# Tiles of 512 bytes and more on 128-byte borders of their SBUF partition

## Chip, cores and metric

The kernel runs on one core of a Trainium2 chip. The metric is the device time of one execution in microseconds (us), as the median of several runs. SBUF has 128 partitions. A tile `[P, n]` of float32 takes 4n bytes at the same place of each partition, and "start" means in all that follows the first byte of such a place modulo 128.

## What is computed

The reference runs x, a 256 x 1024 float32 array, through four blocks: twice the first kind, a final norm, twice the second kind. Cut to what matters:

```python
for l in range(2):                                    # first kind
    x = x + 0.5 * swiglu(rms_norm(x), w_gu, w_down)   # 1024 -> 2 x 2816 -> 1024
    x = x + hybrid_mixer(rms_norm(x))   # gated spatial unit + top-k attention, gated, @ w_out
    x = x + 0.5 * swiglu(rms_norm(x), w_gu, w_down)
x = rms_norm(x)
for l in range(2):                                    # second kind
    h = hybrid_mixer_2(rms_norm(x))     # gated delta rule + dilated attention, @ w_out
    x = x + rms_norm(h)
    h = conv_glu(rms_norm(x))           # up, convolution over 3 tokens, gelu gate, down
    x = x + rms_norm(h)
```

All products are wanted to float32 accuracy.

## The kernel before

Activations lie with features on the partitions and the 256 tokens along the partition, in chunks of 128 features. Weights come from DRAM in slabs of 128 x 1024 (4 KB of each partition) by DMAs that the SP queue issues (`raw`, L179), into four buffers `wraw`.

Each slab is split into two float32r parts: ScalarE writes the rounded part `whi` (`act`, L144), and VectorE and GpSimd write the rest `wlo`, 640 and 384 columns of it (`tt`, L161). Activations are split in the same way into `[P, 2, 256]` tiles: `h` out of the norms, `hid` for the hidden chunks of the feed-forward blocks, `ya`, `yb` and `zh` in the first mixer, `oa` and `ob` in the second.

`mm3_steps` (its product is at L222) makes one 128 x 256 output from 8 such chunks with three products a chunk: `whi` by the first part and `wlo` by the first part in turns, then `whi` by the second part. In each, the 128 x 128 block of the weight slab is loaded into the array as the stationary operand (512 bytes of a partition), and the activation part streams past it as the moving operand (1024 bytes). The trace shows the load as PEld and the product as PE. The load of the next product runs while the present one streams. `token_steps` (L542 to L544) has the roles the other way: 512 columns of the weights move past a block of `h`. Products of plain float32 (transposes, attention scores, the delta rule) have two records of PE each.

A feed-forward stage is an up part (44 slabs of 24 products with `h` as the moving operand) and a down part (8 outputs from 22 chunks, 8 x 66 = 528 products with `hid` moving). There are four SwiGLU stages (`swiglu`) and two with a convolution (`conv_glu`).

**Where tiles start.** A pool (`tc.tile_pool`) hands out places one behind the other, in the order in which names are first asked for. Each place is rounded up to 32 bytes and there are as many places as the name has buffers. Pools open at the same time lie one behind the other. The first pool begins at a multiple of 128. So the starts follow from the code:

- `const`: 352 + 512 + 32 + 64 + 2080 + 32 + 32 + 1024 = 4128 bytes, so that the next pool begins at 32.
- `weights` (4096 x 4 x 3 bytes) and `state`: `wraw`, `whi`, `wlo`, `x`, `sq`, `h`, `ssum`, `rb` start at 32. `state` ends with small tiles of 192 bytes in all, and what follows begins at 96.
- `const1`, `const2` (tables), and the pools `ffn` and `glu`: all start at 96, `t`, `s`, `p`, `y` and `hid` among them.
- `mix1`: `lng`, `ws`, `cosr`, `rm2s`, `k`, `q`, `qi`, `ya` at 96; `rl` and `score` at 32; `yb` and `zh` at 64.
- `mix2`: the 2 KB tiles of the delta rule (`big`, which later hold `obh` and `obl`), `pm2s`, `qT`, `vT`, `sz` at 96; `ct`, `Tf`, `XTf` (later `oa`), `rope` at 64; `kT` and `qg` at 0; `ob` at 32.

A block of a weight slab starts 512 bytes behind the block before it, and the second part of an activation 1024 bytes behind the first, so all blocks and parts of a tile have the tile's start. Of the products of L222, stationary and moving operand therefore start at: `h` 32 and 32; `hid` and `ya` 32 and 96; `yb`, `zh` and `oa` 32 and 64; `ob` 96 and 32.

What sets the order of the work is written in the kernel (`manual_schedule` around the mixers' products) or left to the scheduler of the tile framework. Neither is touched.

Of the kernel before, what the change touches and what calls it, by code (L numbers as in the profile page):

```python
# [7 lines left out]
F32 = mybir.dt.float32  # L8
# [3 lines left out]
PSUM = bass.MemoryType.PSUM  # L12
# [5 lines left out]
P = 128  # L18
T = 256
# [18 lines left out]
# how much other work the tensor engine gets in each wait of the second mixer  # L38
# [4 lines left out]
# columns of the per-partition vectors  # L43
# [5 lines left out]

class Kernel:  # L50
    def __init__(self, tc, ctx, I, out):
        self.tc, self.nc, self.I, self.out = tc, tc.nc, I, out
        pool = lambda **k: ctx.enter_context(tc.tile_pool(**k))
        self.cp = pool(name="const", bufs=1)
        self.wp = pool(name="weights", bufs=4)
        self.sp = pool(name="state", bufs=2)
        self.pp = pool(name="acc", bufs=4, space=PSUM)

    # ---------------------------------------------------------------- the whole
    def run(self, stages=None):  # L60
# [25 lines left out]
        with self.tc.tile_pool(name="const1", bufs=1) as cp:  # L86
            con = self.vec2 = None
            for n, (kind, l) in enumerate(first):
                if n == 1:
                    self.second_constants()  # L90
                v = vec1[:, 8 + V1 * l:8 + V1 * (l + 1)]
                if kind == "mixer1":
                    if con is None:
                        con = {n: self.load(cp, list(I[n].shape), I[n], n)
                               for n in ("cos1", "sin1", "causal0", "causal1")}
                        self.cos1, self.sin1 = con["cos1"], con["sin1"]
                        self.causal = [con["causal0"], con["causal1"]]
                    self.mixer1(l, v)
                else:
                    g = V_FFN1 if kind == "ffn1" else V_FFN2  # L100
                    self.swiglu(v[:, g:g + 8], I[kind + "_gu"][l], I[kind + "_down"][l])
# [3 lines left out]
        with self.tc.tile_pool(name="const2", bufs=1) as cp:  # L105
# [33 lines left out]
    # ---------------------------------------------------------------- small helpers  # L139
# [6 lines left out]
    def turn(self):  # L146
        """Functions of one table come in turns on the scalar engine: what act_next issues from
        here on stays behind what it issued before."""
        self.before, self.latest = self.latest, None
# [32 lines left out]
    def piece(self, src, n, pool_cols=None):  # L182
        """A slab of weights in its two exact float32r parts."""
        if self.plan or self.made:
            while self.plan and len(self.made) < 3:
                self.made.append(self.parts(*self.plan.pop(0)))
            for p in self.plan[len(self.ahead):self.far]:
                self.ahead.append(self.raw(p[0], p[1]))
            return self.made.pop(0)
        return self.parts(src, n, pool_cols)  # L190
# [21 lines left out]
    def mm3(self, ps, w, hs, start=True, stop=True, M=P):  # L212
        """ps[m, t] += W^T h for a slab of len(hs) blocks of M columns."""
# [3 lines left out]
    def mm3_steps(self, ps, w, hs, start=True, stop=True, M=P, shared=False):  # L217
        """The same a product at a time. In a bank shared by two open sums the one that begins first
        has start; that marks the whole bank as unwritten."""
# [14 lines left out]
    def pump(self, us):  # L234
        """Issue that much of the products that wait in the queue."""
# [6 lines left out]
    def split(self, pool, src, name, bufs, lo_eng=None, tag=None):  # L242
        """src (SBUF, float32) in its two float32r parts."""
# [5 lines left out]
    # ---------------------------------------------------------------- normalisation  # L249
# [5 lines left out]
    def square_sum(self, acc, src, **k):  # L255
        """Sum of squares over chunks: a pair of addends, of which the second is the latest."""
# [9 lines left out]
    def rms(self, acc, n):  # L266
        """1/sqrt(mean + eps) by token: on the partitions [128, 2], and along the free axis in PSUM."""
# [3 lines left out]
    def warm(self, n, of=None):  # L271
        """Products for nothing: the tensor engine's clock would halve in a long wait."""
# [16 lines left out]
    def column_sums(self, ps, acc, first, warm=0):  # L289
        """ps[t, b] = sum over the partitions, for the tokens of each block; first: opens the bank."""  # L290
# [14 lines left out]
    def norm(self, g):  # L305
        """x * g in two parts by chunk of features, and 1/rms by token (applied after the product)."""
# [34 lines left out]
    def between(self, gf, g):  # L341
        """x = rmsnorm(x) * gf, then what scaled(g) gives for it; the first norm's scale by token joins
        the second's, so that the products need not wait for either."""
# [27 lines left out]
        def column():  # L371
# [7 lines left out]
            # the mean square of the normed x  # L379
# [15 lines left out]
    def add_normed(self, ys, acc, g=None):  # L395
        """x += rmsnorm(y) * g', for ys = y * g'; then what scaled(g) gives for the new x."""
# [40 lines left out]
    # ---------------------------------------------------------------- gated feed-forward  # L437
    def swiglu(self, g, wgu, wd):
# [3 lines left out]
        with self.tc.tile_pool(name="ffn", bufs=2) as fp:  # L442
# [20 lines left out]
    def open_pairs(self, w, hs, column):  # L463
        """The first two pairs of products, feature chunk by feature chunk as they come from the norm."""
# [19 lines left out]
    def conv_glu(self, vec, wup, wdown, following):  # L484
# [4 lines left out]
        with self.tc.tile_pool(name="glu", bufs=2) as fp:  # L489
# [34 lines left out]
    # ---------------------------------------------------------------- projections  # L524
    def token_layout(self, src, hs, parts=4):
        """The 512 columns of a projection with tokens on the partitions: two banks."""
# [27 lines left out]
    def rotated(self, pool, ps, cs, tag, swaps, m2s):  # L554
        """ps * cos + partner(ps) * sin; the partner rows come by DMA."""
# [11 lines left out]
    # ---------------------------------------------------------------- softmax attention  # L567
    def attention(self, pool, q, k, v, bias, tag, fill=0.0, outs=None, midway=None):
        """8 heads of 64; bias by block of queries: [128, keys]. Out: 4 chunks [c, t] in two parts."""
# [5 lines left out]
        def scores(u):  # L575
            pp, qb, e = u
            nk = P * (qb + 1)
            # two heads on the same rows of the array
# [61 lines left out]
    # ---------------------------------------------------------------- the first block's mixer  # L640
    def selection(self, pool, qi, ki, wt):
        """The bias that keeps, for each query, the top 64 keys by the indexer's score, causally."""
# [32 lines left out]
    def mixer1(self, l, vec):  # L675
# [16 lines left out]
        mp = self.tc.tile_pool(name="mix1", bufs=1)  # L692
        swaps = [(64 * a + 32 * b, 64 * a + 32 * (1 - b), 32) for a in range(2) for b in range(2)]
        with mp as mp:
# [20 lines left out]
            # the indexer: queries, one key, head weights  # L715
# [22 lines left out]
            # the gated spatial unit  # L738
# [36 lines left out]
            # attention over the selected keys  # L775
# [7 lines left out]
            # the gates' products fill the waits  # L783
# [36 lines left out]
    def rows(self, ap, n):  # L820
        """A vector of DRAM on every partition."""
        return bass.AP(tensor=ap.tensor, offset=ap.offset, ap=[[0, P], [1, n]])

    # ---------------------------------------------------------------- the second block's mixer
    def mixer2(self, l, vec, following):
# [15 lines left out]
        with self.tc.tile_pool(name="mix2", bufs=1) as mp, self.tc.manual_schedule(engines={PE}):  # L841
            # keys, beta and decay: feature chunk by feature chunk, as they come from the norm
# [5 lines left out]
            for d in range(KD):  # L848
                for g in sums:
                    next(g), next(g)  # L850
                # the two parts of the weights side by side
# [21 lines left out]
            def silu(y):  # L873
                # the exponentials come before all of these
# [5 lines left out]
            def conv_steps(ps, c0, out, name):  # L880
                """A causal convolution over four tokens, then silu, for two chunks."""
# [61 lines left out]
            # what fills the tensor engine in the waits of the delta rule  # L943
# [45 lines left out]
            def delta_part():  # L989
                for m in range(KD):  # L990
                    w = self.piece(None, 0)
                    # the other half of the weights waits in tiles that the delta rule has left
# [45 lines left out]
class Delta:  # L1038
    """The gated delta rule over chunks of 64 tokens, two chunks to a block of 128."""
# [21 lines left out]
    def inverse_norms(self, x, name):  # L1061
        """1 / |x| by token and head, and x with tokens on the partitions."""
# [15 lines left out]
    def rates(self):  # L1078
        """beta, and the logarithm of the decay"""
# [4 lines left out]
        # softplus(x) = max(x, 0) + log1p(e), e = exp(-|x|), with log1p(e) = 2 atanh(e / (2 + e))  # L1084
# [9 lines left out]
        # beta = 1 / (1 + exp(-b))  # L1094
# [28 lines left out]
    def decays(self):  # L1123
        """exp(G) by token, and the decay from token j (partitions) to token i of a chunk"""
        k, nc, mp, g = self.k, self.nc, self.mp, self.g
        mm, ts = nc.tensor.matmul, nc.vector.tensor_scalar
        # cumulative and whole decay of each chunk
# [24 lines left out]
    def keys(self):  # L1152
        """k.k with the decay, and the keys with tokens on the partitions"""
# [19 lines left out]
    def with_decay(self, out, b, x):  # L1173
        """out[j, h, i] = k_j . x_i * decay / |k_j|"""
# [7 lines left out]
    def inverse(self):  # L1182
        """X = (I + A)^-1 by doubling blocks: X' = X (I - T), T = (A X) o M. Kept are its transpose, by
        which the next is (I - T)^T X^T, and X itself, turned back from it. What stands on the left of
        a product is kept as the diagonal blocks of 128 columns (two chunks on the partitions), the
        rest as the 64 columns of a chunk side by side."""
# [9 lines left out]
        # M with -beta_i / |k_i| by row, and ones on the diagonal, where A has them too: that gives I - T  # L1196
# [47 lines left out]
        # the last level has a block of 32 below the diagonal of each chunk  # L1244
# [66 lines left out]
    def scan(self):  # L1311
        """The recurrence over the four chunks, then the norm of its output by token and head."""
# [101 lines left out]
def _slabs(w):  # L1414
    """[L, K, M] -> [L, M/128, 128 of K, K/128 blocks of 128 columns]"""
# [20 lines left out]
def _cols(v):  # L1436
    """[L, n*128] -> [L, 128, n]"""
# [58 lines left out]
```

## Time and profile before

| | us |
|---|---|
| runs | 2013.04 (median), 2007.71, 2017.61 |
| span of the execution in the profile | 2007.4 |
| PE busy | 1916.0 (95%) |
| PEld busy | 1847.7 (92%) |
| VectorE busy | 1326.9 (66%) |
| GpSimd busy | 1215.6 (61%) |
| ScalarE busy | 988.0 (49%) |

No own time stands beside the profiled execution. Its span is 0.3 us under the fastest of the runs and 5.6 us under their median. Matmuls overlap in the array, so the mean of one PE record (some 280 ns) is longer than the distance from one to the next. That distance is what a stage pays for a product: the length of a stretch without gaps, divided by the number of products in it.

### The profile page before, as it was taken

Reading aid. Unit: us, or ns where it says so; the run is one execution under the profiler, and the core shown is the slowest. Engines: PE = TensorE matmul, PEld = TensorE weight load, DVE = VectorE, ACT = ScalarE, POOL = GpSimd, SP = SyncE. Lnnn points to the kernel's source line nnn. Section 1 sums busy time; section 2 is a strip of 40 time slices with the busy share of each in tenths; the row PEclk is TensorE's granted clock in tenths of the full one; section 3 lists DMA queues with packets and bytes.
Section 4 is the critical chain, followed back from the end, with each engine's and each line's share of the span. In section 5 each row is a group of like instructions: output and inputs, shape, how many; then the busy total and the mean of one; then the engine's idle time right before and its main releaser. Section 6 shows DMA issues by size and latency. Waiting matters only on the chain. (4 is left out here: it accounts for less than half of the span.)

```text
span 2007.4 us, 40107 instructions
## 1 busy us (share of the span) xinstructions
PE 1916.0 (95%) x15468; PEld 1847.7 (92%) x15468; DVE 1326.9 (66%) x2270; ACT 988.0 (49%) x1698; POOL 1215.6 (61%) x957
## 2 busy tenths in 40 slices
PE   9999999899999999999999978999998989999988
PEld 8999889899999999899999978979998989789988
DVE  7665785866656655966766567456885485559862
ACT  5444436444444444455444534554555545455553
POOL 5557475555565565665555757564556767555555
PEclk9999999999999999999999989999999999999999
DMA  7666553655666666555566643242556432235553
GB/s 233 184 179 196 190 170 117 188 170 182 184 191 186 184 184 190 169 170 158 163 184 176 193 143 103 66 130 90 165 166 175 132 121 94 70 109 171 163 165 114
DMA packets 102511, 317.17 MB, mean 158 GB/s; under 512 B 13360, under 2 KB 20912, under 8 KB 102320
## 3 DMA queue, kind: packets, MB, share of 16 engines
q1 hardware_dynamic: 102320, 314.61, 51.2%
q8 instruction: 121, 1.98, 0.4%
q14 instruction: 70, 0.57, 0.1%
HBM read 309.58 MB, written 1.05 MB: 155 GB/s over the span
## 5 line engine op out<-in xcount | busy, mean ns | idle before, releaser
L161 POOL TENSOR_TENSOR wlo<-wraw,whi 128x384 fp32r<-128x384 f32 (+1 forms) x609 | 928.3, 1527 | 501.0 <-ACT whi L144 496.8
L222 PE MATMUL mm<-h,whi 128*128 128x256 f32 x6048 | 1121.0, 286 | 15.4 <-DVE h L333 4.9
L222 PEld LDWEIGHTS mm<-h,whi 128*128 128x128 f32 x6048 | 952.4, 193 | 25.4 <-issue 10.5
L144 ACT ACTIVATE whi<-wraw 128x1024 fp32r<-128x1024 f32 (+2 forms) x611 | 609.7, 1001 | 428.3 <-PE mm L222 169.2
L222 PE MATMUL mm<-h,wlo 128*128 128x256 f32 (+1 forms) x3024 | 753.0, 286 | 21.2 <-DVE wlo L161 15.7
L161 DVE TENSOR_TENSOR wlo<-wraw,whi 128x640 fp32r<-128x640 f32 (+3 forms) x563 | 488.0, 867 | 323.6 <-ACT whi L144 322.5
L222 PEld LDWEIGHTS mm<-h,wlo 128*128 128x128 f32 (+1 forms) x3024 | 582.0, 192 | 28.3 <-DVE wlo L161 22.1
L222 PE MATMUL mm<-hid,whi 128*128 128x256 f32 x2112 | 366.0, 278 | 6.9 <-ACT hid L144 6.1
L222 PEld LDWEIGHTS mm<-hid,whi 128*128 128x128 f32 x2112 | 321.8, 189 | 7.7 <-ACT hid L144 6.5
L222 PE MATMUL mm<-hid,wlo 128*128 128x256 f32 x1056 | 249.9, 278 | 2.7 <-DVE wlo L161 2.7
L222 PEld LDWEIGHTS mm<-hid,wlo 128*128 128x128 f32 x1056 | 199.4, 189 | 3.9 <-DVE wlo L161 3.9
L144 ACT ACTIVATE hid<-p 128x256 fp32r<-128x256 f32 x132 | 55.1, 417 | 182.8 <-DVE p L161 182.7
L164 DVE SCALAR_TENSOR_TENSOR y<-t,vec,y 128x254 f32<-128x254 f32 (+1 forms) x176 | 135.6, 828 | 0.0
L161 DVE TENSOR_TENSOR t<-mm,rb 128x512 f32<-128x512 f32 x132 | 90.6, 687 | 37.9 <-PE mm L222 31.7
L161 DVE TENSOR_TENSOR p<-s,t 128x256 f32<-128x256 f32 x88 | 104.2, 1184 | 2.3 <-ACT s L144 2.3
L161 POOL TENSOR_TENSOR hid<-p,hid 128x256 fp32r<-128x256 f32 x44 | 34.9, 793 | 88.2 <-ACT hid L144 88.2
L161 DVE TENSOR_TENSOR hid<-p,hid 128x256 fp32r<-128x256 f32 x88 | 40.7, 462 | 40.1 <-ACT hid L144 40.1
L161 POOL TENSOR_TENSOR ssum<-ssum,sq 128x256 f32<-128x256 f32 x50 | 49.5, 990 | 12.2 <-ACT sq L144 11.1
L144 ACT ACTIVATE s<-y 128x256 f32<-128x256 f32 x44 | 18.4, 419 | 68.8 <-DVE y L164 68.6
L222 PE MATMUL mm<-zh,whi 128*128 128x256 f32 x256 | 47.6, 287 | 4.5 <-DVE gate L161 1.9
L164 DVE SCALAR_TENSOR_TENSOR h<-x,vec,h 128x256 fp32r<-128x256 f32 x72 | 44.7, 628 | 6.2 <-ACT h L144 5.1
L144 ACT ACTIVATE y<-t,vec 128x256 f32<-128x256 f32 x88 | 47.5, 588 | 1.7 <-DVE t L161 1.7
(296 smaller groups left out, 2045.7 us busy)
## 6 DMA issues: line engine op xcount, KB each, us to landing
wraw<-ffn_gu_in SPq DMA_DIRECT2D x175, 512.0 KB
wraw<-w_in_a_in SPq DMA_DIRECT2D x112, 512.0 KB
wraw<-up_in SPq DMA_DIRECT2D x88, 512.0 KB
wraw<-ffn_down_in SPq DMA_DIRECT2D x64, 512.0 KB
wraw<-down_in SPq DMA_DIRECT2D x32, 512.0 KB
wraw<-ffn_down_in SPq DMA_DIRECT2D x32, 384.0 KB
wraw<-w_in_v_in SPq DMA_DIRECT2D x16, 512.0 KB
wraw<-w_out_in SPq DMA_DIRECT2D x16, 512.0 KB
```

The costliest lines, as they stand in the source:

```text
L144: return self.nc.scalar.activation(out, in_, func, **k)
L161: return (eng or self.nc.vector).tensor_tensor(out, a, b, op=op)
L164: return self.nc.vector.scalar_tensor_tensor(out, a, s, b, op0=op0, op1=op1)
L222: mm = lambda a, b, **f: self.nc.tensor.matmul(ps, a, b, skip_group_check=shared, **f)
```

## The change

A class `Pool` stands before `tile_pool` for all pools in SBUF. It adds up the bytes handed out so far. Ahead of a name whose place has 512 bytes or more it fills up to the next multiple of 128 with a tile that nothing reads or writes, and it fills up the end of the pool in the same way. Smaller tiles stay where they fall. After it, `wraw`, `whi`, `wlo`, `h`, `hid`, `ya`, `yb`, `zh`, `oa`, `ob`, `obh`, `obl` and all other tiles of this size start at 0. No instruction is added, removed, moved or given another shape. Comments and docstrings are gone as well.

```diff
+class Pool:
+    LINE = 128
+
+    def __init__(self, tc, name, bufs=1):
+        self.open, self.bufs = tc.tile_pool(name=name, bufs=bufs), bufs
+        self.at, self.seen, self.pads = 0, set(), 0
+
+    def __enter__(self):
+        self.pool = self.open.__enter__()
+        return self
+
+    def __exit__(self, *e):
+        if e[0] is None:
+            self.pad()
+        return self.open.__exit__(*e)
+
+    def pad(self):
+        n = -self.at % self.LINE
+        if n:
+            self.pads += 1
+            self.pool.tile([P, n // 4], F32, name=f"pad{self.pads}", bufs=1)
+            self.at += n
+
+    def tile(self, shape, dtype, name, tag=None, bufs=None):
+        tag, bufs = tag or name, bufs or self.bufs
+        if tag not in self.seen:
+            self.seen.add(tag)
+            size = -(-4 * int(np.prod(shape[1:])) // 32) * 32
+            if size >= 512:
+                self.pad()
+            self.at += size * bufs
+        return self.pool.tile(shape, dtype, name=name, tag=tag, bufs=bufs)
...
-        pool = lambda **k: ctx.enter_context(tc.tile_pool(**k))
+        pool = lambda **k: ctx.enter_context(Pool(tc, **k))
...
-        self.pp = pool(name="acc", bufs=4, space=PSUM)
+        self.pp = ctx.enter_context(tc.tile_pool(name="acc", bufs=4, space=PSUM))
...
-        with self.tc.tile_pool(name="ffn", bufs=2) as fp:
+        with Pool(self.tc, name="ffn", bufs=2) as fp:
```

The pools `const1`, `const2`, `glu`, `mix1` and `mix2` are changed as `ffn` is.

## Rows read from the trace of the kernel before

**Rows 1.** The page, its first part: busy us, share, instructions

```profile
PE 1916.0 (95%) x15468; PEld 1847.7 (92%) x15468; DVE 1326.9 (66%) x2270; ACT 988.0 (49%) x1698; POOL 1215.6 (61%) x957
```

**Rows 2.** Stretches, L222 alone: bounds, length, busy (x) of PE, PEld, clock, DMA

```profile
408.33:528.28 119.95, 119.95 (x999) 119.95 (x1000) 1.00 0.59 183
528.28:588.14 59.86, 59.86 (x530) 59.83 (x528) 1.00 0.65 192
...
1860.00:1925.00 65.00, 60.81 (x487) 58.78 (x487) 1.00 0.51 161
...
1960.00:1982.00 22.00, 22.00 (x189) 22.00 (x188) 1.00 0.63 186
344.00:354.90 10.90, 10.90 (x99) 10.90 (x98) 1.00 0.51 136
354.90:366.90 12.00, 11.60 (x98) 11.26 (x97) 1.00 0.79 227
367.00:393.30 26.30, 24.46 (x192) 24.05 (x193) 0.94 0.58 175
```

**Rows 3.** Products of L222 by moving tile: ns min/median/max

```profile
L222 PE MATMUL mm<-h,whi x6048: 274/283/561, 6.1 to 1926.5; 128*128 128x256 f32 x195, 128*72 128x256 f32 x1
L222 PE MATMUL mm<-hid,whi x2112: 276/276/581, 139.6 to 1996.1; 128*128 128x256 f32 x192
L222 PE MATMUL mm<-ya,whi x128: 276/276/279, 344.0 to 930.1; 128*128 128x256 f32 x128
L222 PE MATMUL mm<-yb,whi x128: 274/280/357, 354.9 to 941.4; 128*128 128x256 f32 x128
L222 PE MATMUL mm<-zh,whi x256: 276/280/416, 366.9 to 967.1; 128*128 128x256 f32 x128
L222 PE MATMUL mm<-oa,whi x96: 277/280/388, 1327.5 to 1758.4; 128*128 128x256 f32 x96
L222 PE MATMUL mm<-ob,obh x96: 276/278/363, 1351.5 to 1779.3; 128*128 128x256 f32 x96
```

**Rows 4.** Plain float32 products with kT: ns min/median/max

```profile
L1178 PE MATMUL sm<-kT x32: 270/275/275, 1220.7 to 1642.0; 128*128 128x128 f32 x32
L1178 PE MATMUL sm<-qT,kT x32: 275/275/275, 1287.4 to 1707.6; 128*128 128x128 f32 x32
```

**Rows 5.** ScalarE on kT and on sz: ns min/median/max

```profile
L144 ACT ACTIVATE kT<-kT x8: 401/403/420, 1209.6 to 1628.7; 128x256 f32<-128x256 f32 x8
L144 ACT ACTIVATE sz<-sz x8: 400/401/403, 1220.0 to 1699.5; 128x256 f32<-128x256 f32 x8
```

**Rows 6.** Groups by line and shape: busy us, mean ns of one | idle before

```profile
L161 DVE TENSOR_TENSOR t<-mm,rb 128x512 f32<-128x512 f32 x132 | 90.6, 687 | 37.9 <-PE mm L222 31.7 <-ACT rb L144 6.0
L161 DVE TENSOR_TENSOR ct<-mm,rb 128x512 f32<-128x512 f32 x12 | 8.2, 686 | 1.6 <-PE mm L222 1.3
L161 POOL TENSOR_TENSOR rope<-rm,pm2s 128x256 f32<-128x256 f32 x16 | 11.8, 742 | 3.0 <-DMA pm2s<-rm 3.0
L161 POOL TENSOR_TENSOR k<-rm,rm2s 128x256 f32<-128x256 f32 x8 | 6.1, 765 | 10.9 <-DMA rm2s<-rm 10.2 <-DVE wlo L161 0.7
```

**Rows 7.** Waits: who waited for whom, us in total, times, longest

```profile
SPq L179 <- DVE wlo L161: 993.0, 497, 29.5
ACT whi L144 <- DMA wraw<-w_in_a_in: 25.8, 8, 5.5
PE mm L222 <- DVE wlo L161: 18.4, 36, 1.9
```

**Rows 8.** The chain that ended last, second conv_glu: start, us, engine, instruction

```profile
1904.08 1.63 DVE y L164 x3
1910.51 1.63 DVE y L164 x3
1916.94 1.63 DVE y L164 x3
...
1940.62 55.76 PE mm L222 x458
```

More of the change, by code (lines that the diff above doesn't have):

```diff
@@ L85, in run @@
         nc.vector.memset(self.mhalf, -0.5)
-        with self.tc.tile_pool(name="const1", bufs=1) as cp:
+        with Pool(self.tc, name="const1", bufs=1) as cp:
             con = self.vec2 = None
@@ L104, in run @@
         self.pool_cols = POOL_COLS
-        with self.tc.tile_pool(name="const2", bufs=1) as cp:
+        with Pool(self.tc, name="const2", bufs=1) as cp:
             con = {n: self.load(cp, list(I[n].shape), I[n], n)
@@ L488, in conv_glu @@
         rb2 = rb[:, None, :].to_broadcast([P, 2, T])
-        with self.tc.tile_pool(name="glu", bufs=2) as fp:
+        with Pool(self.tc, name="glu", bufs=2) as fp:
             hid = []
@@ L691, in mixer1 @@
                     pass
-        mp = self.tc.tile_pool(name="mix1", bufs=1)
+        mp = Pool(self.tc, name="mix1", bufs=1)
         swaps = [(64 * a + 32 * b, 64 * a + 32 * (1 - b), 32) for a in range(2) for b in range(2)]
@@ L840, in mixer2 @@
         self.plan += [half(m, 0) for m in range(KD)]
-        with self.tc.tile_pool(name="mix2", bufs=1) as mp, self.tc.manual_schedule(engines={PE}):
+        with Pool(self.tc, name="mix2", bufs=1) as mp, self.tc.manual_schedule(engines={PE}):
             psb = self.bank([16, T], "sm")
```

## The prediction

> **What bounds the kernel now.** First the busy times of the engines: PE is busy for 95% of the span and no other engine for more than 66% [rows 1]. No instruction changes, so the change can only act through what the same instructions cost when their operands lie elsewhere, and a nanosecond on each of some 13,000 products is 13 us. Next come stretches of the product line alone, to see where PE runs without gaps. In the up part of a SwiGLU stage it does (119.95 of 119.95 us busy, 999 records), and so in the down part (59.86 of 59.86 us, 528 products by the code; the two further records are the tail of the stretch before) [rows 2]. There a product costs its distance to the next: 119.95/999 = 120.1 ns in the up part (120.3 if its own two edge records are taken off) and 59.86/528 = 113.4 ns in the down part. Both are 128x256 products at the full clock: 256 columns at 2.4 GHz are 106.7 ns, so neither runs at the rate of its columns. The duration of single records shows the same step: median 283 ns with `h` moving, 276 with `hid` and `ya`, 280 with `yb`, `zh`, `oa`, 278 with `ob` [rows 3]. Seven ns of duration go with seven of distance.
>
> Not everything is bound by PE. In the second conv_glu's up part PE works 60.81 of 65 us [rows 2], and the chain that ended last runs there over VectorE's `y`, one pair of slabs every 6.43 us; then 55.76 us are PE's alone, the down part [rows 8]. Weights are not late: SP's queue stands 993 us waiting for VectorE to free a slab, while PE waits 18.4 us in all for `wlo` [rows 7].
>
> **What the steps go with.** I set the medians beside the starts that the code gives. Stationary and moving both at 32 (`h`): 283. At 32 and 96, 64 bytes apart (`hid`, `ya`): 276. At 32 and 64, 32 apart (`yb`, `zh`, `oa`): 280. At 96 and 32, 64 apart again (`ob`): 276 at least and 278 in the median [rows 3]. As distances: 120.1, 113.4, about 117 (the rows of `yb` and `zh` lie between the two others, with gaps of their own) [rows 2]. At 1.2 GHz, PE's lower level and half its rate, these are 144, 136 and 140 cycles against 128 for the columns: steps of four. That is too even for chance contention with DMA or other engines, whose load differs from stretch to stretch. It looks like two streams meeting: the next block is loaded while the present activation streams, and the loss is largest where both begin at the same start. I take the difference of the two starts as what counts. Against the moving start alone speaks `ob`: it moves from 32 as `h` does, and runs like those that stand 64 apart. The same stage is not rigid, though: the last down part has 189 records in 22.00 us, 187 without the edges, or 117.6 ns, with the very starts of the 113.4 [rows 2]. So a pair 64 apart has two patterns, and a restart can pick the worse.
>
> **The change part by part.** After it every operand of L222 begins at 0, every pair has the same start, and all should cost what `h` costs now, 120.1 ns. This value is taken from the nearest row, the only pair with equal starts in float32r; bounds from the other rows are 113.4 (nothing lost) and below, which is the second rival.
>
> - `h` (9072 products, also the 512-column ones of the token rows): equal before, equal after. 0.
> - Four SwiGLU down parts: 528 x (120.1 - 113.4) = 3.5 us each, PE without a gap before and after, so all of it reaches the end: +14.2. If they now run in the worse pattern of the last down part at times and the true loss is counted from 117.6 it is 528 x 2.5 x 4 = +5.3, the lower bound.
> - First conv_glu's down part: 528 x 6.7 = 3.5, of which I leave 0.5 to gaps at its start: +3.0. Second: 458 products on the chain [rows 8] from 117.6: 458 x 2.5 = +1.1.
> - First mixers: `ya` 192 products x 6.7 = +1.3; `yb` 192 x 3 = +0.6; `zh` 384 x 3 = 1.2, with PE busy 24.46 of 26.30 us there [rows 2], so +0.8.
> - Second mixers: `oa` and `ob`, 2 x 144 products x 3 to 5 ns, partly in gaps: +0.5.
> - Up parts of conv_glu: bound by VectorE's chain, and `h` does not change: 0.
> - Plain float32 products: with `kT` at 0 on both sides 275 ns, with `qT` at 96 against `kT` at 0 275 too [rows 4]. Their starts cost nothing now and will cost nothing. 0.
> - ScalarE, VectorE, GpSimd: ScalarE takes 403 ns on `kT` (start 0) and 401 on `sz` (96) [rows 5]; VectorE 687 into `t` (96) and 686 into `ct` (64), GpSimd 742 into `rope` (64) and 765 into `k` (96) [rows 6]. The first two show no effect; GpSimd's 3% would at best shorten an engine that has the slack, and its two rows read different tables. 0, between -1 and +1 us.
> - DMA: slabs land at 0 instead of 32. No row has a transfer to another start. A cheaper or dearer landing is covered by the 993 us for which the queue waits for free slabs; if that cover were gone, ScalarE's split of a slab would wait for its DMA in the steady stages, which it now does for only 25.8 us in one input group [rows 7]. 0, up to +2.
> - Pads: some hundred bytes in all. Where a pool opens on the place of a closed one, a tile can overlap another old tile than before and wait for it; such joints are some ten, a fraction of a us each. 0 to +1.
>
> Sum: 14.2 + 3.0 + 1.1 + 1.3 + 0.6 + 0.8 + 0.5 = +21.5 us. On the profiled span, 2007.4, it gives 2029; the median of the runs lies 5.6 us above that span, and on it, 2013.0, the sum gives 2034. Its own range: +9 (the lower bound of the down parts with the rest halved) to +25 (all gaps filled, +2 of DMA and pads), and the 5 us by which the runs scatter on either side: 2019 to 2042.
>
> **The rivals.** *Faster: the start itself costs, not the difference.* If a moving stream loses cycles by its distance to the next 128-byte border (32: 16 cycles, 64: 12, 96: 8), a start at 0 would lose four or none. For it: the order of `h`, `zh` and `hid`, and that two streams from separate readers need not meet at all. Against: `ob`, 278 instead of 283 from 32 [rows 3]; it would need the stationary start at 96 to give back what the moving one costs. It decides if `h` falls below 120. At the best rate of the trace, 113.4, the four SwiGLU up parts give 4 x 1056 x 6.7 = 28 us; `h` in the mixers is 2700 products, and 6.7 ns on each is 18 us, of which about half stands beside gaps: 9. The conv_glu up parts give nothing, VectorE bounds them [rows 8]. Together -37: 1976. At 106.7, the columns' own rate, twice that and a further 528 x 6.7 x 5 = 18 from the down parts: some 1920.
>
> *No change: the step goes with something else* (the pool in which a tile lies, which engine wrote it, which neighbours run), or the pads are counted wrongly and starts stay as they were. For it: `h` differs from `hid` in its writer and place too. Against: `ya` and `yb` lie side by side in one pool with one kind of writer, and have 276 and 280. Time 2013, 2005 to 2019. The Trainium skill speaks for this one ("SBUF — State Buffer", Who interferes with whom): PE has one read port for the moving operand and an independent one for the weights' load, and waits on no one. By it, load and stream could not meet, and the forecast's +21.5 would be 0. The trace agrees in so far as PE's pace holds while DMA and three engines are busy, but the rule has no room for 283 beside 276.
>
> **How the numbers follow.** The forecast fits seven operands with one rule and needs one assumption, that 0/0 behaves as 32/32: 0.60. Faster needs `ob` explained away: 0.20. No change: 0.20. The predicted time is the forecast's, 2034; its own range is 2019 to 2042. For eight in ten the range must take in no change as well: 2005 to 2042, leaving the faster case out. Half a per cent, 10 us, is about what a measurement of this kernel can tell from no change. The forecast's lower bound, +9, lies just inside that, which I don't split off.
>
> **What would show it.** Right: with `hid` and `ya` moving the median record goes from 276 to 283 and a SwiGLU down part from 59.86 to 63.4 us; `yb`, `zh`, `oa`, `ob` come to 283; `h` stays at 283 and its up parts at 119.95; ScalarE's and VectorE's means stay; conv_glu's pairs stay at 6.43 us. Wrong: `h` under 283 and an up part shorter than 119 us mean that the start itself counts; `hid` still at 276 means that the starts were not the cause. A longer 6.43 or a wait of ScalarE for slabs in the steady stages would mean that an engine or a DMA feels the starts after all.

## The result and the profile after

The changed kernel takes 2035.26 us in the median of 4 runs, against 2012.64 for the kernel before; the ratio is 1.0104 (95% interval 1.008 to 1.0128). The forecast was 2034. It is slower by some 22 us, though each large tile now begins on a 128-byte border and no instruction differs.

The profiled execution has a span of 2035.0 us. Its first part has the columns of [rows 1]: busy us, share, number of instructions.

```profile
PE 1944.2 (96%) x15468; PEld 1875.2 (92%) x15468; DVE 1324.1 (65%) x2270; ACT 986.9 (48%) x1698; POOL 1215.6 (60%) x957
```

Same counts as in [rows 1]; PE is 28.2 us busier, its loads (PEld) 27.5, and no other engine changed by more than 2.8. So the time is on PE's own path. Which products, the stretches of the product line show (as in [rows 2]: bounds, length, busy and count of PE, of PEld, clock, DMA share, GB/s): the second SwiGLU stage's up and down parts, then `ya`, `yb` and `zh` of the first mixer.

```profile
414.93:534.88 119.95, 119.95 (x1000) 119.95 (x1001) 1.00 0.59 183
534.88:598.24 63.36, 63.36 (x530) 63.31 (x528) 1.00 0.61 182
351.33:362.72 11.39, 11.39 (x99) 11.39 (x97) 1.00 0.52 139
362.72:374.20 11.48, 11.48 (x98) 11.45 (x96) 1.00 0.69 215
374.77:400.30 25.53, 23.71 (x191) 23.18 (x192) 1.00 0.62 184
```

The up part keeps its pace: 119.95 us hold 1000 records, where they held 999. The down part took 59.86 us and takes 63.36: 63.36/528 = 120.0 ns from product to product, 6.6 more than before. `ya` went from 10.90 to 11.39, `yb` hardly moved. The products by moving tile (ns min/median/max, as [rows 3]) say it record by record:

```profile
L259 PE MATMUL mm<-h,whi x6048: 274/283/582, 6.3 to 1953.2; 128*128 128x256 f32 x195, 128*72 128x256 f32 x1
L259 PE MATMUL mm<-hid,whi x2112: 278/283/583, 142.1 to 2023.8; 128*128 128x256 f32 x192
L259 PE MATMUL mm<-ya,whi x128: 274/281/287, 351.3 to 945.3; 128*128 128x256 f32 x128
L259 PE MATMUL mm<-yb,whi x128: 277/283/283, 362.7 to 956.8; 128*128 128x256 f32 x128
L259 PE MATMUL mm<-zh,whi x256: 280/283/415, 374.8 to 984.3; 128*128 128x256 f32 x128
L259 PE MATMUL mm<-oa,whi x96: 278/283/388, 1347.8 to 1785.0; 128*128 128x256 f32 x96
L259 PE MATMUL mm<-ob,obh x96: 279/283/364, 1371.6 to 1806.1; 128*128 128x256 f32 x96
```

Six of seven stand at 283 now. `ya` has 281, which the forecast's rule does not explain: its start modulo 128 is 0 like the others'.

What was forecast to stay did stay. The chain that ended last (start, us, engine, line) still goes over VectorE's `y` every 6.43 us in the last conv_glu, and the last down part (458 products on the chain) is 56.71 us instead of 55.76 [rows 8]:

```profile
1924.34 1.62 DVE y L201 x3
1930.77 1.62 DVE y L201 x3
...
1967.34 56.71 PE mm L259 x458
```

VectorE, GpSimd and SP's queue, in the groups by line and the waits ([rows 6, 7]):

```profile
L198 DVE TENSOR_TENSOR t<-mm,rb 128x512 f32<-128x512 f32 x132 | 90.6, 687 | 39.6 <-PE mm L259 32.1 <-ACT rb L181 7.4
L198 POOL TENSOR_TENSOR rope<-rm,pm2s 128x256 f32<-128x256 f32 x16 | 11.8, 743 | 3.1 <-DMA pm2s<-rm 3.1
L198 DVE TENSOR_TENSOR ct<-mm,rb 128x512 f32<-128x512 f32 x12 | 8.2, 685 | 1.6 <-PE mm L259 1.3
```
```profile
SPq L216 <- DVE wlo L198: 1015.3, 506, 29.9
```

687, 743 and 685 ns against 687, 742 and 686: in these groups VectorE and GpSimd do not feel where a tile begins. Nor does ScalarE: its rounding of a whole slab takes 1052 ns after 1053 and its operation on `sz`, which moved from 96 to 0, 401 as before. The queue waits 22 us longer for free slabs, about the length that the kernel has gained.

Two more stretches, of the kernel before (the first conv_glu's down part; 15 to 20 us) and then of the changed one:

```profile
1511.75:1579.10 67.35, 62.56 (x529) 61.56 (x528) 0.97 0.63 187
15.00:20.00 5.00, 4.46 (x35) 4.31 (x36) 1.00 0.94 272
```
```profile
1532.17:1603.82 71.65, 67.18 (x530) 66.17 (x528) 0.95 0.59 176
15.00:20.00 5.00, 3.64 (x18) 3.57 (x18) 0.53 0.88 260
```

Where the 27.6 us between the two profiled spans lie: four SwiGLU down parts, 4 x 3.5 = 14.0; the first conv_glu's down part 4.3; the last one 0.95; `ya` twice 0.5. A further 2.4 us are the first up part's, where PE came to its full clock later: 0.53 between 15 and 20 us, 1.00 in the kernel before. The kernel with `hid` taken back, below, had the same (0.53), the one with `hid` padded in the kernel before had not (1.00). Nor had the ones with all activations or with everything at 64 (1.00 each), so the late clock does not follow from aligned tiles alone; whether these 2.4 us belong to the change or to single executions is not settled. The rest, some 5 us, is spread over the mixers in pieces of up to 1.9, of both signs. The medians differ by only 22.6: 5 of the 27.6 us come from which executions were profiled, a short one before and one 1.5 us above its median after.

### The profile page after: what moved, and what is told of

Its sections match the earlier page's. It is cut to its first block, busy times and chain, and to the rows that moved or that the text cites. A ratio compares the mean times of both kernels' runs of the same rounds, so it can differ in the third digit from the quotient of the medians.

```text
span 2035.0 us, 40107 instructions
## 1 busy us (share of the span) xinstructions
PE 1944.2 (96%) x15468; PEld 1875.2 (92%) x15468; DVE 1324.1 (65%) x2270; ACT 986.9 (48%) x1698; POOL 1215.6 (60%) x957
## 5 line engine op out<-in xcount | busy, mean ns | idle before, releaser
L259 PEld LDWEIGHTS mm<-h,wlo 128*128 128x128 f32 (+1 forms) x3024 | 583.7, 193 | 28.2 <-DVE wlo L198 22.3
L259 PE MATMUL mm<-hid,whi 128*128 128x256 f32 x2112 | 385.9, 285 | 6.8 <-ACT hid L181 6.0
L259 PEld LDWEIGHTS mm<-hid,whi 128*128 128x128 f32 x2112 | 333.4, 194 | 7.6 <-ACT hid L181 6.4
L259 PE MATMUL mm<-hid,wlo 128*128 128x256 f32 x1056 | 262.1, 285 | 2.1 <-DVE wlo L198 2.1
L259 PEld LDWEIGHTS mm<-hid,wlo 128*128 128x128 f32 x1056 | 204.2, 193 | 3.3 <-DVE wlo L198 3.3
```

What stands on the lines that cost most here:

```text
L259: mm = lambda a, b, **f: self.nc.tensor.matmul(ps, a, b, skip_group_check=shared, **f)
```

## Experiments

Three theories are set against each other. A is the prediction's: the difference of the two starts counts. B: the moving start alone counts. C: something else that goes with a tile counts, its pool, its writer or its neighbours.

### Products alone

```diff
...
+                for g, (w, m) in enumerate(ORDER_):
+                    ps = self.bank([P, T])
+                    n = 96
+                    for k in range(n):
+                        s = slice(P * (k % 8), P * (k % 8) + P)
+                        t = slice(T * (k // 8 % 2), T * (k // 8 % 2) + T)
+                        nc.tensor.matmul(ps, W[w][:, s], M[m][:, t], start=k == 0, stop=k == n - 1)
...
```

> A kernel with nothing but 128x256 float32r products: one slab of eight stationary blocks at start 0, 32, 64 or 96 against one moving activation at 0, 32, 64 or 96, 96 products of each of the 16 pairs, all of it twice (the second time in reverse order), and in between 0 against 4, 8, 16, 24, 40, 48, 56, 72, 80, 112, 128, 192, 256 and 512, and 32 against 128 and 512. It leaves out the whole of the reference's computation. Theory A (the difference of the two starts counts): 120.0 ns from product to product wherever the starts are equal, 116.7 where they are 32 apart, 113.4 where they are 64 apart, whatever the absolute starts; 96 apart, which no product of the kernel before has with this sign, is 32 apart the other way round and gives 116.7. Theory B (the moving start alone counts, 0 and 32 being equally dear): 120 for moving starts 0 and 32, 116.7 for 64, 113.4 for 96 with every stationary start. Theory C (pool, writer or neighbours): no difference between the pairs. For differences above 128 A expects the value of the difference modulo 128; for those that are no multiple of 32 it has no number of its own, between the neighbours.

Stretches of this kernel (length, busy and count of PE, PEld, VectorE, ScalarE, GpSimd; clock, DMA share, GB/s). In order: equal starts 0/0, 32/32, 64/64, 96/96; weights 0 with 64; weights 96 with 32, in the first and in the second pass; weights 0 with 128; weights 0 with 112.

```profile
401.82:413.34 11.52, 11.52 (x98) 11.52 (x97) 0.42 (x1) 0.00 (x0) 0.00 (x0) 1.00 0.01 1
94.80:106.30 11.50, 11.50 (x98) 11.50 (x97) 0.42 (x1) 0.00 (x0) 0.00 (x0) 1.00 0.01 1
151.17:162.69 11.52, 11.52 (x99) 11.52 (x97) 0.42 (x1) 0.00 (x0) 0.00 (x0) 1.00 0.01 1
208.06:219.57 11.51, 11.51 (x98) 11.51 (x97) 0.42 (x1) 0.00 (x0) 0.00 (x0) 1.00 0.00 0
60.62:71.93 11.31, 11.31 (x98) 11.31 (x97) 0.42 (x1) 0.00 (x0) 0.00 (x0) 1.00 0.00 1
185.39:196.70 11.31, 11.31 (x98) 11.31 (x97) 0.42 (x1) 0.00 (x0) 0.00 (x0) 1.00 0.01 1
436.21:447.13 10.92, 10.92 (x99) 10.92 (x97) 0.42 (x1) 0.00 (x0) 0.00 (x0) 1.00 0.00 0
333.25:344.63 11.38, 11.38 (x98) 11.38 (x97) 0.42 (x1) 0.00 (x0) 0.00 (x0) 1.00 0.01 1
322.32:333.25 10.93, 10.93 (x98) 10.93 (x97) 0.42 (x1) 0.00 (x0) 0.00 (x0) 1.00 0.01 1
```

Each stretch is 96 products (the counts take in the edges). Equal starts cost 11.51/96 = 119.9 ns at all four absolute starts, where B wanted 113.4 with the moving start at 96, so B falls. So does C, which wanted no difference between pairs: here all tiles have one writer and one pool, and no neighbour is at work. The loss is there with DMA at 0.01 and the other engines idle, so no other engine and no DMA causes it. But A is only half right. A wanted 113.4 for starts 64 apart. Weights 0 with 64 cost 117.8, and weights 96 with 32 first 117.8 and later 113.8, in one execution. And 128 apart is not like 0: 11.38/96 = 118.5, while 256 and 512 apart gave 120.0 again. So the difference counts modulo 256 (96 with 32 is then 192, not 64), and some differences have more than one speed. Read in this way from the code, the moving operand stood behind the stationary one by 0 (`h`), 192 (`hid`, `ya`), 32 (`yb`, `zh`, `oa`) and 64 (`ob`) in the kernel before. In the changed kernel it is 0 for all of them but `ya`, which stands at 128.

### All activations 64 away

```diff
+    START = {'h': 64, 'hid': 64, 'ya': 64, 'yb': 64, 'zh': 64, 'ob': 64, 'Tf': 64, 'XTf': 64}
+    REST = 0
...
-    def pad(self):
-        n = -self.at % self.LINE
+    def pad(self, start=0):
+        n = (start - self.at) % self.LINE
...
-                self.pad()
+                self.pad(self.START.get(tag, self.REST))
```

> The changed kernel, but all activations that move or stand as float32r operands (h, hid, ya, yb, zh, ob, and the places Tf and XTf in which oa lies) start at 64, the weights stay at 0. Theory A (difference): every pair is 64 apart and costs 113.4 ns, all medians of the product line are 276 ns, a SwiGLU up part shortens from 119.95 to 113.3 us and a down part stays at 59.86 as before. Against the kernel before: 4 x 1056 x 6.7 ns = -28, h in the mixers -9 to -18, the small ones -2, conv_glu's up parts nothing: 1960 to 1975 us. Theory B (moving start alone): 280 ns everywhere, h 3.3 ns cheaper than before (-14 and -5 in the mixers), hid 3.4 dearer (+8): about 2002. Theory C: as the changed kernel, 2035.

2005.34 us, 0.996 of the kernel before (0.9938 to 0.9982): shorter, but by 7 us where A said 38 to 53. Stretches of the product line: the last 119.96 us of the third SwiGLU up part, and the first and third down parts.

```profile
593.07:713.03 119.96, 119.76 (x1017) 119.58 (x1016) 1.00 0.60 184
137.80:199.98 62.18, 62.18 (x530) 62.18 (x529) 1.00 0.62 182
713.03:772.88 59.85, 59.85 (x530) 59.85 (x529) 1.00 0.64 188
```

The up part holds 1017 products where it held 1000: 118.0 ns, not 113.4. And two down parts with the same starts differ, 117.8 against 113.4 ns. Modulo 256 `h` stands at 64 here and `hid` at 192. The expectation took one of the two speeds for the rule.

### Only `hid`, in the kernel before

```diff
+                if j == 0:
+                    fp.tile([P, 16], F32, name="move", bufs=1)
                 hid.append(self.split(fp, p, "hid", NF))
```

The same pad stands in conv_glu.

> The kernel before with one pad of 64 bytes ahead of hid in each feed-forward pool, so that hid alone moves from 96 to 32, the start of the weights; everything else stays where it was. Theory A and the working of the prediction: the down parts pay 120.0 instead of 113.4, 14.2 + 3.0 + 1.1 = +18 us, 2031. B (moving start alone) gives the same here. Theory C: no change, 2013. If the 22 us that the change cost came in a larger part from the other aligned tiles, from the DMAs or from the pads, this run falls well short of 2031.

2032.12 us, 1.0098 (1.007 to 1.0126). One pad of 64 bytes in front of `hid`, in the kernel without any alignment, costs 19.5 us of the change's 22.6. Products by moving tile:

```profile
L222 PE MATMUL mm<-hid,whi x2112: 279/283/583, 139.9 to 2022.0; 128*128 128x256 f32 x192
L222 PE MATMUL mm<-ya,whi x128: 276/276/279, 349.5 to 941.7; 128*128 128x256 f32 x128
```

`hid` is at 283; `ya`, which stayed, is at 276. Pool, writer and neighbours of `hid` are as before, so this too speaks against C.

### Everything at 64

As the kernel with all activations at 64, but with these two lines:

```diff
+    START = {}
+    REST = 64
```

> The changed kernel with all tiles of 512 bytes and more at 64 instead of 0. Theory A: all differences are 0 as after the change, all medians 283 ns, 2035 us. Theory B: moving start 64, 280 ns everywhere, 3.3 ns less for each of the products that PE bounds (some 7,500): about 2010. A rival for the prediction's assumption that 0 against 0 behaves as 32 against 32: that a multiple of 128 is itself the bad start; then 2013 or less.

2029.44 us, 1.0085 (1.0054 to 1.0116). Products by moving tile, and the third up part's last 119.96 us:

```profile
L261 PE MATMUL mm<-h,whi x6048: 274/282/582, 6.2 to 1944.2; 128*128 128x256 f32 x195, 128*72 128x256 f32 x1
L261 PE MATMUL mm<-hid,whi x2112: 276/283/420, 138.6 to 2014.8; 128*128 128x256 f32 x192
```
```profile
602.57:722.53 119.96, 119.96 (x1000) 119.96 (x1000) 1.00 0.60 183
```

`hid`, moving from 64, has 283: B's 280 is refuted, and a multiple of 128 is not the bad start. `h` has 282. It lies 128 behind the weights modulo 256 here, as `ya` does in the changed kernel (281), and that is how the odd row above is read. It is no gain of pace in the up part, which still holds 1000 products in 119.96 us. The median is 6 us under the changed kernel's, but the two intervals (1.0054 to 1.0116 and 1.008 to 1.0128) overlap, so it is not shown that this kernel is the faster of the two.

### Products alone, every 16 bytes

```diff
...
+                for g, m in enumerate(ORDER_):
+                    ps = self.bank([P, T])
+                    hi, lo = M[m][:, :T], M[m][:, T:]
+                    steps = [(W[w], k, hi) for k in range(KD) for w in ("hi", "lo")] + [(W["hi"], k, lo) for k in range(KD)]
+                    steps = 4 * steps
...
```

> Only 128x256 float32r products again, now in the kernel's own order (24 of a slab: first part with whi and wlo in turns, second part with whi, four times over), both weight tiles at 0 modulo 256, one activation at each multiple of 16 bytes modulo 256 and at 8, 104, 120, 136, 232 and 248, four times each in shuffled orders. It leaves out the whole of the reference's computation. After the first four runs theory A is amended to A2: the difference counts modulo 256, not 128 (the h of the kernel with all tiles at 64 and the ya of the changed kernel stand 128 apart modulo 256 and show 118.6 and not 120.0 ns). A2 expects 120.0 at 0, 118.6 at 128, 117.8 or 113.4 at 64 and 192, between 116 and 120 at the other multiples of 32. Where a difference has two values, the product before decides which; with four different predecessors both should be seen at 192. A expects 0 and 128 to be equal, and one value for each difference. Whether some difference always gives 113.4 or less is open.

Stretches of 96 products, the columns as above, with the activation at 0, 64, 96, 112, 128 and 192 behind the weights:

```profile
185.51:197.01 11.50, 11.50 (x99) 11.50 (x97) 0.42 (x1) 0.00 (x0) 0.00 (x0) 1.00 0.01 1
242.30:253.60 11.30, 11.30 (x98) 11.30 (x97) 0.42 (x1) 0.00 (x0) 0.00 (x0) 1.00 0.01 1
94.44:105.95 11.51, 11.51 (x99) 11.51 (x97) 0.42 (x1) 0.00 (x0) 0.00 (x0) 1.00 0.01 1
276.75:287.65 10.90, 10.90 (x99) 10.90 (x97) 0.42 (x1) 0.00 (x0) 0.00 (x0) 1.00 0.01 2
```

```profile
151.07:162.46 11.39, 11.39 (x98) 11.39 (x97) 0.42 (x1) 0.00 (x0) 0.00 (x0) 1.00 0.00 1
117.47:128.36 10.89, 10.89 (x98) 10.89 (x97) 0.42 (x1) 0.00 (x0) 0.00 (x0) 1.00 0.00 0
```

In ns a product: 120.0 at 0, 117.8 at 64, 120.0 at 96, 113.5 to 113.9 at 112, 118.7 at 128, 113.4 to 113.7 at 192, in all four stretches of each; the others lie between 116.6 and 121.3. That agrees with the amended rule at 0 and 128, and 96 apart is no mirror of 32 apart as A had it. Not as expected, 192 showed only the faster of its two speeds here, after four different predecessors. Over both kernels 112 had 113.5 to 113.9 in six of six stretches, 64 had 117.8 in eight of eight, and 192 had 113.4 to 113.8 in seven of ten and 117.8 in three. Differences of 16 and 32 had three speeds each, 113.3, 116.7 and 118.7 and 116.7, 117.8 and 120.0.

### Only `hid` taken back, in the changed kernel

```diff
+    START = {'whi': 0, 'wlo': 0, 'big': 0, 'h': 0, 'hid': 192}
...
-    def pad(self):
-        n = -self.at % self.LINE
+    def pad(self, start=0, line=256):
+        n = (start - self.at) % line
...
-                self.pad()
+                self.pad(*((self.START[tag], 256) if tag in self.START else (0, self.LINE)))
```

> The changed kernel with hid alone taken from 0 to 192 modulo 256 behind the weights, where the kernel before has it (and oa, which nothing hangs on, at 128). All other tiles stay on their 128-byte borders. If the down parts of the feed-forward stages carry the loss, and if 192 gives 113.4 in all four SwiGLU stages as it does in the kernel before, 18 of the 22 us come back: 2016. If the pattern of 117.8 is as likely there as in the kernel with all activations at 64 (two of four stages), half of it: 2024. If the loss lies in the other tiles, in DMAs or pads: 2035.

2015.55 us, 1.0015 (0.9998 to 1.0032): within the error of the kernel before. 19.7 of the 22.6 us come back, with all other tiles still on 128-byte borders. Pads, DMAs and the other tiles together are thus worth some 3 us, by the interval between 0 and 6. The second up and down parts:

```profile
411.42:531.37 119.95, 119.95 (x999) 119.95 (x1000) 1.00 0.58 183
531.37:591.13 59.76, 59.76 (x530) 59.76 (x528) 1.00 0.64 192
```

### All activations at 192

As the run before, with another table:

```diff
+    START = {'whi': 0, 'wlo': 0, 'big': 0, 'h': 192, 'hid': 192, 'ya': 192, 'yb': 192, 'zh': 192, 'ob': 192, 'Tf': 192, 'XTf': 192}
```

> The changed kernel with all float32r activations at 192 modulo 256 behind the weights. If the difference of 192 always gave 113.4: h falls from 120.0 to 113.4 in the four SwiGLU up parts and the mixers, 1970 to 1980 us. If it falls into 117.8 as h does at a difference of 64: about 2005, as in the kernel with all activations at 64 modulo 128, and stages differ among each other. By theory B (moving start alone): also 2005, but all stages alike.

2006.86 us, 0.9957 (0.9942 to 0.9972). The second down part, and the third:

```profile
527.46:589.54 62.08, 62.08 (x530) 62.08 (x528) 1.00 0.63 186
715.24:777.32 62.08, 62.08 (x530) 62.08 (x529) 1.00 0.61 182
```

`hid` stands 192 behind the weights in this run and in the one before it, and takes 117.8 ns a product here and 113.4 there, in all four SwiGLU stages of either run (62.07 and 59.75 us from first to last product). What runs just ahead of it differs: `h` at 192 instead of 0. So the speed of a stretch may hang on what ran before it, but no run isolates this. Nor is it the whole: in the kernel with all activations at 64 two of the four down parts took 117.8 and two 113.4, after like up parts. The SwiGLU stages do not differ among each other as expected, but `ya`, also at 192, has a median of 276 ns while `h` and `hid` have 281. B, with one moving start for all three, does not allow that.

### Activations at 112

Pools hand out multiples of 32 bytes. So the places of `hid`, `ya` and `yb` are 256 bytes longer and are used from their 16th byte on, and the eight buffers of `h` lie in one tile, also 16 bytes on:

```diff
+    SHIFT = {'hid': 4, 'ya': 4, 'yb': 4}
+    ONE = {'h': 4}
+    START = {'whi': 0, 'wlo': 0, 'big': 0, 'h': 96, 'hid': 96, 'ya': 96, 'yb': 96, 'zh': 192, 'ob': 192, 'XTf': 192, 'Tf': 192}
...
+        e = self.SHIFT.get(tag)
+        if e:
+            t = self.pool.tile([P, n + 64], dtype, name=name, tag=tag, bufs=bufs)
+            return t[:, e:e + n].rearrange("p (a b) -> p a b", a=shape[1])
...
+            t, i = self.one[tag]
+            self.one[tag][1] = (i + 1) % bufs
+            return t[:, e + n * i:e + n * i + n].rearrange("p (a b) -> p a b", a=shape[1])
```

> The changed kernel with h, hid, ya and yb at 112 modulo 256 behind the weights, and zh, oa and ob at 192. The products alone showed 113.3 to 113.9 ns at 112 in six of six stretches, after six different predecessors; no other difference did that (192 had it in some and 117.8 in others). If that holds in the kernel: h falls from 120.0 to 113.4, four SwiGLU up parts 4 x 1056 x 6.7 = -28 us, h in the mixers -5 to -15, conv_glu's up parts nothing (VectorE), the down parts as in the kernel before: 1970 to 1982 us, and a SwiGLU up part of 119.95 us becomes 113.3. If the change of the slab after each 8 blocks or 24 products knocks it into the other pattern, as with 64 and 192: 2000 to 2008. If VectorE or the slabs' DMAs become the bound of the up parts: PE shows gaps there, in between.

1985.25 us, 0.9854 of the kernel before (0.9838 to 0.9871): the fastest of all, 30 us under the kernel before and 50 under the changed one, though 3 us above the expected 1970 to 1982. The third up part's last 113.32 us, and the third down part; then the products:

```profile
582.72:696.04 113.32, 113.32 (x1000) 113.32 (x1000) 1.00 0.62 192
696.04:755.79 59.75, 59.75 (x530) 59.75 (x529) 1.00 0.65 191
```
```profile
L274 PE MATMUL mm<-h,whi x6048: 275/275/561, 6.3 to 1901.2; 128*128 128x256 f32 x195, 128*72 128x256 f32 x1
L274 PE MATMUL mm<-hid,whi x2112: 275/275/581, 133.1 to 1970.3; 128*128 128x256 f32 x192
```

A thousand products in 113.32 us instead of 119.95, without a gap: neither VectorE nor the slabs' DMAs became the bound there. Four up parts, from first to last product, are 26.7 us shorter. The medians differ by 30 and the spans of the two profiled executions by 25.8, so the mixers, where 5 to 15 us were expected, gave 3 at most. It seems that what their products save falls into their gaps.

## Why the prediction was right

- **Equal starts cost 120.1, whatever they are.** Right, and shown at 0, 32, 64 and 96 in the products alone.
- **Four down parts, +14.2.** 4 x 3.5 = 14.0. The padded `hid` alone brought 19.5 us of loss, the restored `hid` alone took 19.7 back: the six down parts, four SwiGLU and two conv_glu, carry the change.
- **conv_glu's down parts, +3.0 and +1.1.** 4.3 and 0.95. The 0.5 that the forecast left to gaps hid nothing, and the first stretch also ran at a granted clock of 0.95 where it had 0.97 before. In the kernel with everything at 64, where `hid` has equal starts too and the clock was 0.98, the same stretch took 70.5 us, 3.1 more than before; so the rest of the 4.3 goes with the clock.
- **First mixers, +2.7.** `ya` gave 1.0 of 1.3, since it went to 128 behind the weights and so to 118.6 ns; `yb` 0.2 of 0.6 (11.33 to 11.38 and 11.21 to 11.39 us from first to last product). `zh` was 0.8 shorter in the first mixer and 1.8 longer in the second, but the clock differs too: 0.94 was granted in the first mixer before (26.30 us) and in the second after (26.82), 1.00 in the two others (25.05 before, 25.53 after). At like clocks `zh` is 0.5 longer, twice: 1.0 where 0.8 was forecast.
- **`oa` and `ob`, +0.5.** From first to last product `ob` is 0.3 us longer in each second mixer and `oa` 0.3 and 0.1 shorter: +0.2. The sum took 144 products of each; there are 192.
- **float32, ScalarE, VectorE, GpSimd, DMA, pads, conv_glu's up parts at about nothing.** Right for the rows shown, the plain float32 products of `qT` with `kT` included (275 ns again, now both at 0). DMA and pads have no row of their own; the kernel with `hid` taken back bounds them.
- **The sum, +21.5.** The parts add up to some 21.6 in the two profiled executions. That this is so close is in part luck: the first conv_glu's extra 1.3, most of which is not the price of its products, makes up for what `ya`, `yb`, `oa` and `ob` fell short. The ends of the forecast's own range are slightly off its own terms (2013 + 9 - 5 is 2017 and not 2019, 2013 + 25 + 5 is 2043 and not 2042); the result lies well inside either.
- **What was not right, though it cost the sum only 0.3 us (`ya`).** Starts were read modulo 128 and a pair 64 apart was given 113.4 as its speed, with a worse pattern as an accident of a restart. The difference counts modulo 256, and at 192, where `hid` and `ya` stood, 113.4 is one of two speeds. The kernel before had the better one in its SwiGLU stages, and as the forecast took its price from those very stages, the price held. That 64 modulo 256 costs 117.8 is why the expectation for all activations at 64 missed by 30 us and more.
- **The rivals.** No change is refuted by the single pad before `hid`. The faster one (the start itself counts) is refuted by the four equal pairs. Its price for `h`, 28 us in the up parts and 9 in the mixers, was paid out by another cause, the difference of 112, as 27 and 3 at most. The Trainium skill's rule ("SBUF — State Buffer", Who interferes with whom), by which the weights' read and the moving read have independent ports and PE waits on no one, leaves no room for 113.3 to 120 ns from nothing but the two starts; the measurement decides. That the load of the next block meets the running stream is a reading that fits, but it is argued and not shown: no row shows the place where they would meet.

## What to carry to other kernels

Where TensorE runs without gaps, the distance from product to product is worth dividing out for each pair of operands: here 113, 118 and 120 ns stood side by side for one shape, and the cause was where two tiles begin. Aligning everything gave all pairs but one the same start and so the slow pace; what helped was to place the moving tile at a chosen distance, 112 bytes modulo 256, behind the stationary one and to keep it over all buffers. A pad elsewhere in a pool can undo it, so the starts are to be looked up after each change of the tiles.

## What the runs showed of the hardware

At the full clock a 128x256 float32r product costs 113.3 to 123.2 ns when nothing but the starts of its two operands changes and no other engine is at work; what counts is their difference modulo 256. At 0 it was 120.0 everywhere, at 64 117.8, at 112 113.5 to 113.9 (113.3 in a whole up part), at 128 118.7, though 120.0 in a whole up part. The steady SwiGLU stages of the full kernel show 113.3 to 120.0. At 192 there are two speeds, 113.4 and 117.8, which hold over whole stages of 528 products. What chooses between them stays open; in two kernels it went with the start of the products just before. VectorE, GpSimd and ScalarE showed nothing of it in the groups read here.
